# Later transposes between the stages, lo parts of just-in-time weights on GpSimd, and a bonus term computed one step later

## The chip, the cores and the metric

The kernel runs on one core of one Trainium2 chip, in one launch. The metric is the device time of that launch in microseconds (us), median of several runs. One execution was also profiled, and every duration below is from it.

## The reference

A batch of one sequence of 512 tokens with 1024 features goes through two transformer layers and then through one further block. All of it is float32.

```python
# layers i = 0 (latent and windowed attention), 1 (attention with forget gates)
x = layer_norm(ALPHA * x + mixer_i(x), ln1)            # mixer ends in  o @ w_out
x = layer_norm(ALPHA * x + relu(x @ w_up)**2 @ w_down, ln2)
x = x + sigmoid(x @ ple_w_gate + b) * (p[i] @ ple_w_proj)
# the second block
h = rms_norm(x); proj = h @ w_in
a = rwkv7(h, r, k, v)      # recurrence; adds bonus = sum_head(r * k * r_k) * v
c = conformer_conv(...)
x = x + (gate0 * (a @ w_rp) + gate1 * (c @ w_cp)) @ w_o
x = x + relu(rms_norm(x) @ w_ff1)**2 @ w_ff2
return rms_norm(x)
```

## The kernel before

**Numbers.** Each float32 product is made of three TensorE matmuls on rounded parts: hi x hi, hi x lo, lo x hi (`mm3`, line 285). Every weight tile (128 x 1024) is brought by SyncE's DMA queue into a `wraw` buffer, ScalarE writes its hi part, and the lo part, raw - hi, is made in one of two ways (`load_part`, line 257). Without a named engine, ScalarE writes -hi and GpSimd issues a DMA that adds raw to it (lines 266, 267). With one, that engine subtracts (line 269). `fast=True` takes VectorE and GpSimd in turn and overrides the named engine.

**Layout.** The residual x is token-major: four tiles of 128 tokens x 1024. A product needs its other operand feature-major, X = (hi, lo), 8 x 128 features by 512 tokens. `to_fm` (line 337) brings one token block there: 2 x 4 transposes on TensorE into two psum banks, then hi by ScalarE and lo by VectorE (lines 348, 349).

**Handovers.** A mixer ends in `out_proj` (line 534): four columns of 256, in each column four token blocks (one step = 24 matmuls of 256 columns), and an addition to x on VectorE per step. In the last column, `after(tb - 1)` follows step tb and `after(3)` follows the loop; `after` is a norm and then `to_fm` of that block (`norm_after`, line 551). `second_mixer` does the same by hand (lines 1254 to 1269), with all its transposes in the one bank psq. The next phase, `ffn` (line 400), begins with `up(0)`, whose two products are made in token halves (`halves=i == 0`, line 421); all its up-projection weights have their lo parts made by GpSimd (line 418). It ends in `down_last` (line 505), where `after(tb - 1)` follows the step of block tb, and `after(3)` follows `fill`, a small product of the gate phase. The gate phase (line 615) makes two columns of 512, the first with `fast`, the second through ScalarE and DMA.

**Recurrence.** In the second block eight feature chunks pass through four generators, a chunk a round further in each (lines 1211 to 1236): `wkv_proj`, `wkv_inputs`, `wkv_inverse`, `wkv_chunks`. `interleave` writes their steps in turn by the numbers they yield. `wkv_inputs` ends with the bonus (lines 1475 to 1480): r x r_k x k on VectorE, a sum per head on TensorE, and a product with v on VectorE. `wkv_inverse` inverts triangular blocks with a round trip through DRAM, and makes three token-major copies by transposes (lines 1554 to 1566); each has four copies out of psum, two on ScalarE and two on VectorE.

**Order.** The order in the program is a priority. A planner with a cost model places each instruction in its engine's queue, may move a ready one ahead of one that isn't ready, and inserts the semaphores; on the chip each engine takes its queue in order. Buffers of a tag (`bufs`) are handed on when their last reader is done.

Of the kernel before, what the change touches and what calls it, by code (L numbers as in the profile page):

```python
# [19 lines left out]
D = 1024  # L20
LOW = -3.0e38
DECAY_C = -0.5 * math.exp(-0.5)
HALVES = slice(0, 512), slice(512, 1024)


# [264 lines left out]

def proj_fm(g, W, X, m0, tag="psm", halves=False):

    ps = g.ps(tag)
    n = len(W)
    for t0, t1 in (((0, 256), (256, 512)) if halves else ((0, 512),)):
        for kc in range(n):
            w = tuple(a[:, m0:m0 + 128] for a in W[kc])
            mm3(g.nc, ps[:, t0:t1], w, (X[0][:, kc, t0:t1], X[1][:, kc, t0:t1]), kc == 0, kc == n - 1)
    return ps
# [36 lines left out]

def to_fm(g, src, X, tb, tag="psm"):

    nc = g.nc
    for half in range(2):  # L340
# [58 lines left out]

def ffn(g, w_up, w_down, X, alpha, hp, tmp, after, fill=None):  # L400

# [11 lines left out]
    QS = {k: hp.tile([128, 2, 512], F32, name=f"q{k}", tag=f"q{k}", bufs=1) for k in (5, 6, 7)}  # L413

    def up(i):

        plain = i // 2 == units - 1
        W = g.load_w(w_up[:, i * 256:i * 256 + 256], eng=nc.gpsimd)
        F = tmp.tile([128, 8, 256], F32, name="hf", tag="hf")
        for e in range(2):  # L420
            p3 = proj_fm(g, W, X, e * 128, halves=i == 0).rearrange("p (a t) -> p a t", a=2)
# [107 lines left out]
    if fill:  # L529
        fill()  # L530
    after(3)


def out_proj(g, w, Ws, X, alpha, tag, after, order=None):

    nc = g.nc
    for c in range(4):  # L540
        W = Ws[c] if c < len(Ws) else g.load_w(w[:, c * 256:c * 256 + 256])
        for tb in range(4):
            ps = proj_tm(g, W, X, tb, tag, order)
            xs = g.x[tb][:, c * 256:c * 256 + 256]
            nc.vector.scalar_tensor_tensor(xs, xs, alpha, ps[:, 0:256], op0=ALU.mult, op1=ALU.add)
            if c == 3 and tb > 0:
                after(tb - 1)
    after(3)


def norm_after(g, pool, l, which, X, tag):

    gb, bb = g.bcast_row(pool, f"{which}_g{l}", f"{which}g"), g.bcast_row(pool, f"{which}_b{l}", f"{which}b")

    def after(tb):
        layer_norm_tm(g, g.x[tb], gb, bb)
        to_fm(g, g.x[tb], X, tb, tag)

    return after


def ffn_and_ple(g, l, X):

    nc, tc, d = g.nc, g.tc, g.d
    with ExitStack() as s2:
# [16 lines left out]
        with ExitStack() as s3:  # L582
            hp = g.pool(s3, "hp", 3)
            tmp = g.pool(s3, "ftmp", 1)
            br = g.pool(s3, "brow", 1)
            after = norm_after(g, br, l, "ln2", X, "psm")
            P = []
# [4 lines left out]

            ffn(g, d[f"w_up{l}"], d[f"w_down{l}"], X, ALPHA, hp, tmp, after, fill)
        tmp = g.pool(s2, "ptmp", 3, side="right")
# [130 lines left out]
def even_mixer(g, outer, late, X, load_x):  # L725
    d, nc = g.d, g.nc
    with ExitStack() as st:
# [25 lines left out]
        for j in order:  # L753
            split_sb(g, OT[:, j, :], X[0][:, j, :], X[1][:, j, :], nc.vector)
        out_proj(g, d["ev_w_out"], W, X, ALPHA, "pss", norm_after(g, g.pool(st, "evn", 1), 0, "ln1", X, "pst"), order)

# [229 lines left out]
def odd_mixer(g, late, X):  # L986
    nc, tc, d = g.nc, g.tc, g.d
    with ExitStack() as st:
# [55 lines left out]
        g.weight_pools(late, *FFN_W, side="right")  # L1044
        out_proj(g, d["od_w_out"], W, X, ALPHA, "pss", norm_after(g, g.pool(st, "odn", 1), 1, "ln1", X, "pst"))

# [4 lines left out]
def first_block(g):  # L1051
# [22 lines left out]
    with ExitStack() as st:  # L1074
        g.small = g.pool(st, "small", 6)
        for l in range(2):
            with ExitStack() as late:
                if l == 0:
                    even_mixer(g, st, late, X, load_x)
                else:  # L1080
                    odd_mixer(g, late, X)
                ffn_and_ple(g, l, X)

# [12 lines left out]
def second_mixer(g, outer):  # L1096
    nc, tc, d = g.nc, g.tc, g.d
    H = g.X
    with ExitStack() as st:
# [150 lines left out]
        g.small = g.pool(outer, "small2", 6, side="right")  # L1250
        hn = g.pool(st, "hn2", 2)
        gb = g.bcast_row(hn, "norm_ff")

        def after(tb):
            ht = hn.tile([128, D], F32, name="hn2", tag="hn2")
            rms_norm_tm(g, g.x[tb], ht, gb, g.v1[:, V1["eps6"][0]:V1["eps6"][1]])
# [4 lines left out]
        for cc in range(4):  # L1261
            W = g.load_w(d["w_o"][:, cc * 256:cc * 256 + 256]) if cc else W
            for tb in range(4):
                ps = proj_tm(g, W, H, tb, ("psm", "pst")[tb % 2])
                xs = g.x[tb][:, cc * 256:cc * 256 + 256]
                nc.vector.scalar_tensor_tensor(xs, ps[:, 0:256], 0.5, xs, op0=ALU.mult, op1=ALU.add)
                if cc == 3 and tb > 0:
                    after(tb - 1)
        after(3)


# [133 lines left out]
def wkv_inputs(g, fc, st, env):  # L1405
# [81 lines left out]
def wkv_inverse(g, fc, st, env):  # L1487
# [198 lines left out]
def second_block(g, out):  # L1686
    nc, tc, d = g.nc, g.tc, g.d
    with ExitStack() as st:
        with ExitStack() as s2:
            g.psum(s2, psm=3, psd=1, pst=2, psq=1, pso=1)  # L1690
            second_mixer(g, st)
        g.psum(st, psa=4, psu=2, psm=2)
# [4 lines left out]

        def after(tb):
            ht = tmp.tile([128, D], F32, name="hn2", tag="hn2", bufs=3)
# [3 lines left out]

        ffn(g, d["w_ff1"], d["w_ff2"], g.X, 1.0, hp, tmp, after)

# [20 lines left out]
```

## Time and profile before

| | |
|---|---|
| median of 3 runs | 2544.66 us (2542.65 to 2544.73) |
| profiled execution, its own time | 2543.96 us |
| its span, first to last instruction | 2542.2 us |
| TensorE busy | 94% |
| VectorE, ScalarE, GpSimd busy | 60%, 50%, 40% |

The profile names PE (TensorE), PEld (its weight loads), DVE (VectorE), ACT (ScalarE), POOL (GpSimd) and SP (SyncE). A wait is put down to the work that released it. PEclk is the TensorE clock that was granted, 1.00 being the full 2.4 GHz.

### The profile page before, as it was taken

How to read it: one execution, taken by the hardware profiler on the slowest of the kernel's cores; microseconds unless marked ns; L12 is line 12 of the kernel's file. 1: busy time of each engine (PE TensorE's matmuls, PEld its weight loads, DVE VectorE, ACT ScalarE, POOL GpSimd, SP SyncE). 2: the span in 40 equal slices, each digit the busy share in tenths (PEclk: the TensorE clock that was granted, in tenths of full speed). 3: DMA queues.
4: the chain of work that ended last, by engine and by line, in shares of the span. 5: the costliest groups of instructions: out<-in, count | busy, mean ns of one | idle time of the engine just before them, and what ended most of it. 6: DMA issues, size and time to landing. Idle time of an engine off the chain costs nothing.

```text
span 2542.2 us, 36431 instructions
## 1 busy us (share of the span) xinstructions
PE 2381.3 (94%) x14140; PEld 1909.5 (75%) x14140; DVE 1531.6 (60%) x2834; ACT 1273.4 (50%) x1963; POOL 1028.3 (40%) x567
## 2 busy tenths in 40 slices
PE   8998999999999998999999988999998999799998
PEld 6778777787777787877877866777766778677776
DVE  3775464667343646565684697877767542555656
ACT  5782544445455644444445443555556533354543
POOL 1113667661011024767621332323354223367672
PEclk9999999999999999999999998999999999899999
DMA  7455232336555262232363565656675459132422
GB/s 207 89 154 162 67 112 88 108 123 158 147 125 122 62 166 88 71 121 79 115 171 93 123 151 124 150 130 136 137 175 145 133 171 258 41 116 73 125 70 82
DMA packets 303214, 315.35 MB, mean 124 GB/s; under 512 B 61376, under 2 KB 235072, under 8 KB 302912
## 3 DMA queue, kind: packets, MB, share of 16 engines
q1 hardware_dynamic: 280432, 239.60, 31.1%
q0 software_dynamic: 22032, 71.31, 15.6%
q8 instruction: 111, 1.82, 0.3%
q10 hardware_dynamic: 576, 2.10, 0.2%
q14 instruction: 63, 0.52, 0.1%
HBM read 221.47 MB, written 20.19 MB: 95 GB/s over the span
## 4 chain that ended last, share of the span: by engine, by line
PE 54%; DVE 15%; issue 9%; POOL 8%; DMA 8%; ACT 6%; SPq 0%; POOLq 0%; DVEq 0%; ACTq 0%
PE psm L286 7%; PE psm L287 7%; PE psm L288 7%; DMA wlo<-wraw 4%; PE psa L286 3%; PE psa L287 3%; PE psa L288 3%; POOL wlo L386 3%; DVE hl L386 2%; PE pst L1385 2%; PE psd L286 2%; DVE cacc L1376 2%; PE psd L288 2%; PE pss L287 2%; PE pss L288 2%
## 5 line engine op out<-in xcount | busy, mean ns | idle before, releaser
L286 PE MATMUL psm<-xT,whi 128*128 128x512 f32 (+1 forms) x1288 | 505.6, 393 | 20.8 <-DVE ksl L721 9.0
L287 PE MATMUL psm<-xT,whi 128*128 128x512 f32 (+1 forms) x1288 | 498.9, 387 | 1.4 <-DVE xT L349 1.4
L288 PE MATMUL psm<-xT,wlo 128*128 128x512 f32 (+1 forms) x1288 | 496.6, 386 | 3.0 <-DMA wlo<-wraw 3.0
L267 POOL DMA_DIRECT2D wlo<-wraw x153 | 132.6, 868 | 834.3 <-ACT wlo L266 560.3
L263 ACT ACTIVATE whi<-wraw 128x1024 fp32r<-128x1024 f32 (+3 forms) x287 | 286.2, 1005 | 334.8 <-PE psa L288 101.1
L386 POOL TENSOR_TENSOR wlo<-wraw,whi 128x1024 fp32r<-128x1024 f32 x84 | 214.3, 2552 | 282.9 <-ACT whi L385 282.9
L269 POOL TENSOR_TENSOR wlo<-wraw,whi 128x1024 fp32r<-128x1024 f32 x112 | 291.3, 2631 | 60.8 <-ACT whi L263 60.3
L286 PEld LDWEIGHTS psm<-xT,whi 128*128 128x128 f32 x1288 | 246.6, 192 | 73.5 <-issue 12.0
L288 PEld LDWEIGHTS psm<-xT,wlo 128*128 128x128 f32 x1288 | 247.0, 192 | 50.8 <-DMA wlo<-wraw 4.1
L287 PEld LDWEIGHTS psm<-xT,whi 128*128 128x128 f32 x1288 | 247.7, 192 | 46.8 <-DVE xT L349 2.6
L286 PE MATMUL psa<-whi,hh 128*128 128x512 f32 x600 | 239.1, 399 | 17.2 <-DVE x L443 17.0
L287 PE MATMUL psa<-wlo,hh 128*128 128x512 f32 x600 | 236.7, 395 | 0.0
L288 PE MATMUL psa<-whi,hl 128*128 128x512 f32 x600 | 236.5, 395 | 0.0
L385 ACT ACTIVATE whi<-wraw 128x1024 fp32r<-128x1024 f32 x147 | 151.6, 1053 | 127.0 <-PE psa L288 62.1
L1376 DVE SCALAR_TENSOR_TENSOR cacc<-glu,cw,cacc 128x512 f32<-128x512 f32 x240 | 199.4, 831 | 5.4 <-ACT cacc L1373 1.3
L386 DVE TENSOR_TENSOR hl<-hf,hh 128x768 fp32r<-128x768 f32 (+1 forms) x96 | 124.3, 1295 | 60.3 <-ACT hh L385 60.3
L385 ACT ACTIVATE hh<-hf 128x768 fp32r<-128x768 f32 (+1 forms) x96 | 87.7, 914 | 143.7 <-DVE hf L434 142.0
L286 PEld LDWEIGHTS psa<-whi,hh 128*128 128x128 f32 x600 | 112.8, 188 | 51.9 <-DVE x L443 25.1
L386 DVE TENSOR_TENSOR wlo<-wraw,whi 128x1024 fp32r<-128x1024 f32 x63 | 90.7, 1464 | 94.3 <-ACT whi L385 80.2
L266 ACT ACTIVATE wlo<-whi 128x1024 fp32r<-128x1024 f32 (+2 forms) x153 | 146.3, 960 | 2.3 <-PE psm L288 0.8
L288 PEld LDWEIGHTS psa<-whi,hl 128*128 128x128 f32 x600 | 112.8, 188 | 27.3 <-DVE hl L386 0.7
L287 PEld LDWEIGHTS psa<-wlo,hh 128*128 128x128 f32 x600 | 112.8, 188 | 25.8
(445 smaller groups left out, 5113.0 us busy)
## 6 DMA issues: line engine op xcount, KB each, us to landing
wlo<-wraw POOLq DMA_DIRECT2D x129, 512.0 KB, 5.4
wraw<-in_w_up SPq DMA_DIRECT2D x64, 512.0 KB, 4.5
wraw<-in_w_down SPq DMA_DIRECT2D x64, 512.0 KB, 3.5
wraw<-in_w_ff SPq DMA_DIRECT2D x64, 512.0 KB, 3.7
wraw<-in_w_in SPq DMA_DIRECT2D x56, 512.0 KB, 4.4
wraw<-in_od_w_in SPq DMA_DIRECT2D x24, 512.0 KB, 4.3
wraw<-in_ple_w_gate SPq DMA_DIRECT2D x16, 512.0 KB, 5.6
brow<-in_rows SPq DMA_DIRECT2D x13, 512.0 KB, 5.4
```

Of the source, the lines that this page charges most:

```text
L263: nc.scalar.activation(hi[:, :m], raw[:, :m], AF.Copy)
L266: nc.scalar.activation(lo[:, :m], hi[:, :m].bitcast(F32), AF.Copy, scale=-1.0)
L267: nc.gpsimd.dma_start(lo[:, :m].bitcast(F32), raw[:, :m], accum_op=ALU.add)
L269: eng.tensor_tensor(lo[:, :m], raw[:, :m], hi[:, :m].bitcast(F32), op=ALU.subtract)
L286: nc.tensor.matmul(ps, w[0], x[0], start=first, stop=False)
L287: nc.tensor.matmul(ps, w[0], x[1], start=False, stop=False)
L288: nc.tensor.matmul(ps, w[1], x[0], start=False, stop=last)
L385: g.nc.scalar.activation(hi, src, AF.Copy)
L386: (eng or g.nc.gpsimd).tensor_tensor(lo, src, hi.bitcast(F32), op=ALU.subtract)
L1376: nc.vector.scalar_tensor_tensor(acc, u[:, j:j + 512], cw[:, fc * 31 + j:fc * 31 + j + 1], acc, op0=ALU.mult, op1=ALU.add)
L1385: nc.tensor.matmul(ps[o], lhs[o], rhs[o], start=start, stop=stop)
```

## The change

In `out_proj` and `second_mixer` the columns 2 and 3 are made together for one token block, its norm follows at once, and the transposes follow two blocks later. The transposes of blocks 2 and 3 are returned as callables (`late`) and run inside the next phase: in `up(0)` between its half products, in the gate phase between its first steps. The first two up-projection weights take the way through ScalarE and DMA; weights of an output projection that are loaded inside the loop, and those of the second gate column, have their lo part made by GpSimd. In the recurrence, `wkv_inputs` makes only r x r_k x k, and sum and product run in `wkv_inverse` while its DRAM round trip is under way; the four copies per transposed tile all go to ScalarE. The buffers hn2 move to a longer-lived pool.

```diff
+LATE_TAGS = "pst", "psm"
+HALF_TOKENS = slice(0, 256), slice(256, 512)
 def ffn(...):                      # after -> late, norm, fm
+    def first_two(W):
+        pss = [g.ps("psm") for _ in range(2)]
+        for half, t in enumerate(HALF_TOKENS):
+            for e, ps in enumerate(pss):
+                for kc in range(8):
+                    w = tuple(a[:, e * 128:e * 128 + 128] for a in W[kc])
+                    mm3(nc, ps[:, t], w, (X[0][:, kc, t], X[1][:, kc, t]), kc == 0, kc == 7)
+                if half == 0:
+                    late[e]()
+        return pss
     def up(i):
-        W = g.load_w(w_up[:, i * 256:i * 256 + 256], eng=nc.gpsimd)
+        W = g.load_w(w_up[:, i * 256:i * 256 + 256], eng=nc.gpsimd if i > 1 else None)
     # down_last, behind the addition of block tb:
-                if c == 1 and tb > 0:
-                    after(tb - 1)
+                if c == 1:
+                    norm(tb)
+                    if fm and tb > 1:
+                        fm(tb - 2)
...
-    after(3)
+    return [functools.partial(fm, tb) for tb in (2, 3)] if fm else None
+def columns(g, w, Ws, step, norm, fm):        # out_proj and second_mixer call it
+    load = lambda c: Ws[c] if c < len(Ws) else g.load_w(w[:, c * 256:c * 256 + 256], eng=g.nc.gpsimd)
+    for c in range(2):
+        W = load(c)
+        for tb in range(4):
+            step(W, c, tb)
+    W2, W3 = load(2), load(3)
+    for tb in range(4):
+        step(W2, 2, tb)
+        step(W3, 3, tb)
+        norm(tb)
+        if tb > 1:
+            fm(tb - 2)
+    return [functools.partial(fm, tb, ("psa", "psa")) for tb in (2, 3)]
 # gate phase
-            Wg = g.load_w(d[f"ple_w_gate{l}"][:, cs], fast=c == 0)
+            Wg = g.load_w(d[f"ple_w_gate{l}"][:, cs], fast=c == 0, eng=nc.gpsimd)
             for tb in range(4):
+                if c == 0 and 0 < tb < 3:
+                    late[tb - 1]()
 # second_mixer: transposes of block tb
-            to_fm(g, ht, H, tb, "psq")
+            to_fm(g, ht[tb], H, tb, tags or (("psq", "pso"), ("psd", "psq"))[tb])
 # wkv_inputs
-    rk = tmp("tmpa")
-    nc.vector.scalar_tensor_tensor(rk, r, col(vv("r_k"), fc), k, op0=ALU.mult, op1=ALU.mult)
-    ps = g.ps("psm")
-    nc.tensor.matmul(ps, c("blk"), rk, start=True, stop=True)
     bon = new("bon", bufs=3)
-    nc.vector.tensor_tensor(bon, ps, v, op=ALU.mult)
+    nc.vector.scalar_tensor_tensor(bon, r, col(vv("r_k"), fc), k, op0=ALU.mult, op1=ALU.mult)
 # wkv_inverse, behind the issue of the round trip's last DMAs
+    ps = g.ps("psm")
+    nc.tensor.matmul(ps, c("blk"), st["bon"], start=True, stop=True)
+    nc.vector.tensor_tensor(st["bon"], ps, st["v"], op=ALU.mult)
+    yield 1.0
...
-                eng = nc.scalar.copy if hp == 0 else nc.vector.tensor_copy
-                eng(tv[64 * hp:64 * hp + 64, :, cp, :], p4[64 * cp:64 * cp + 64, :, hp, :])
+                nc.scalar.copy(tv[64 * hp:64 * hp + 64, :, cp, :], p4[64 * cp:64 * cp + 64, :, hp, :])
```

## Rows read from the trace of the kernel before

**Rows 1.** The page: busy time of each engine, share of the span, instructions.
```profile
PE 2381.3 (94%) x14140; PEld 1909.5 (75%) x14140; DVE 1531.6 (60%) x2834; ACT 1273.4 (50%) x1963; POOL 1028.3 (40%) x567
```

**Rows 2.** Stretches: us, busy us of each engine (instructions), PEclk, DMA share, GB/s.
```profile
210.00:218.00 8.00, 8.00 (x69) 8.00 (x68) 1.26 (x3) 1.06 (x1) 2.74 (x2) 1.00 0.90 255
...
2185.40:2193.40 8.00, 7.99 (x44) 7.99 (x45) 0.00 (x0) 0.00 (x0) 0.00 (x0) 0.61 0.17 61
...
226.00:257.00 31.00, 23.99 (x173) 21.86 (x172) 24.47 (x36) 10.38 (x17) 11.34 (x5) 0.94 0.11 33
...
1316.00:1328.00 12.00, 7.56 (x37) 5.10 (x36) 12.00 (x16) 6.57 (x11) 6.93 (x4) 1.00 0.87 216
...
2120.00:2140.00 20.00, 16.24 (x114) 15.74 (x113) 2.55 (x6) 8.98 (x10) 3.31 (x5) 0.83 1.05 285
...
640.00:650.00 10.00, 9.53 (x31) 7.26 (x32) 2.08 (x3) 0.63 (x1) 0.00 (x0) 0.73 0.84 195
...
1460.00:1480.00 20.00, 14.48 (x50) 10.58 (x50) 19.00 (x25) 7.91 (x11) 9.10 (x7) 0.83 0.68 150
```

**Rows 3.** TensorE's waits (total, times, longest): 226 to 257, 944 to 973, 2165 to 2203.
```profile
PE pst L344 <- issue: 3.3, 2, 1.8
PE pst L344 <- DVE bmv L368: 2.1, 1, 2.1
...
PE pst L344 <- DVE x L372: 2.7, 2, 1.4
PE pst L344 <- DVE bmv L368: 2.0, 1, 2.0
...
PE psq L344 <- DVE xT L349: 11.1, 4, 4.7
```

**Rows 4.** TensorE's waits, 900:916, 2120:2140, 630:650, 1354:1361; DMA landings (page, chain).
```profile
PE pss L287 <- DMA wlo<-wraw: 1.9, 2, 1.2
...
PE psm L287 <- DMA wlo<-wraw: 3.8, 2, 2.7
...
PE psa L287 <- DMA wlo<-wraw: 4.7, 3, 3.0
...
PE psa L287 <- DMA wlo<-wraw: 2.5, 2, 1.7
...
wlo<-wraw POOLq DMA_DIRECT2D x129, 512.0 KB, 5.4
...
2121.41 10.40 DMA wlo<-wraw
```

**Rows 5.** TensorE's waits at the two gates, 588 to 606 and 1316 to 1328.
```profile
PE psm L344 <- DVE x L372: 3.2, 2, 1.9
...
PE psm L344 <- DVE x L372: 3.5, 2, 1.8
```

**Rows 6.** TensorE's waits 1440 to 1560; line L1564, duration ns min/median/max.
```profile
PE psm L1478 <- DVE tmpa L1476: 5.5, 1, 5.5
PE pst L1557 <- DVE vtk L1564: 5.0, 1, 5.0
...
L1564 ACT COPY vtk<-pst x16: 348/369/371, 1519.1 to 2002.9; 64x256 f32<-64x256 f32 x16
...
L1564 DVE COPY vtk<-pst x16: 417/422/428, 1531.4 to 2003.3; 64x256 f32<-64x256 f32 x16
```

**Rows 7.** Timeline near 600 (start, us); line L371, duration ns min/median/max.
```profile
601.46 2.67 POOL L269 TENSOR_TENSOR wlo<-wraw,whi 128x1024 fp32r<-128x1024 f32 x1
...
590.08 1.41 DVE L372 SCALAR_TENSOR_TENSOR x<-x,rs,brow 128x512 f32<-128x512 f32 x2
...
601.55 3.80 DVE L372 SCALAR_TENSOR_TENSOR x<-x,rs,brow 128x512 f32<-128x512 f32 x2
...
L371 DVE SCALAR_TENSOR_TENSOR x<-x,bmv,brow x32: 727/747/2924, 223.5 to 1324.1; 128x512 f32<-128x512 f32 x32
```

More of the change, by code (lines that the diff above doesn't have):

```diff
@@ L1 @@
+import functools
 import itertools
@@ L288, in mm3, with proj_fm @@
     nc.tensor.matmul(ps, w[1], x[0], start=False, stop=last)
-def proj_fm(g, W, X, m0, tag="psm", halves=False):
+def proj_fm(g, W, X, m0, tag="psm"):
     ps = g.ps(tag)
     n = len(W)
[L295 to L298, printed above, removed]
+    for kc in range(n):
+        w = tuple(a[:, m0:m0 + 128] for a in W[kc])
+        mm3(g.nc, ps, w, (X[0][:, kc, :], X[1][:, kc, :]), kc == 0, kc == n - 1)
     return ps
@@ L334, in proj_tm, with to_fm @@
     return ps
-def to_fm(g, src, X, tb, tag="psm"):
+def to_fm(g, src, X, tb, tags=("psm", "psm")):
     nc = g.nc
-    for half in range(2):
+    for half, tag in enumerate(tags):
         ps = g.ps(tag)
@@ L397, with ffn @@
 BLOCK = {1: 0, 2: 1, 3: 6, 4: 2, 5: 3, 6: 4, 7: 5}
-def ffn(g, w_up, w_down, X, alpha, hp, tmp, after, fill=None):
+def ffn(g, w_up, w_down, X, alpha, hp, tmp, late, norm, fm=None, fill=None):
     nc = g.nc
@@ L530, in ffn, with out_proj, step, norm_fm @@
         fill()
-    after(3)
[L534 to L541, printed above, removed]
-        for tb in range(4):
[L543 to L551, printed above, removed]
-    gb, bb = g.bcast_row(pool, f"{which}_g{l}", f"{which}g"), g.bcast_row(pool, f"{which}_b{l}", f"{which}b")
[L555 to L562, printed above, removed]
+    return [functools.partial(fm, tb) for tb in (2, 3)] if fm else None
+def out_proj(g, w, Ws, X, alpha, tag, norm, fm, order=None):
+    def step(W, c, tb):
+        ps = proj_tm(g, W, X, tb, tag, order)
+        xs = g.x[tb][:, c * 256:c * 256 + 256]
+        g.nc.vector.scalar_tensor_tensor(xs, xs, alpha, ps[:, 0:256], op0=ALU.mult, op1=ALU.add)
+    return columns(g, w, Ws, step, norm, fm)
+def columns(g, w, Ws, step, norm, fm):
+    load = lambda c: Ws[c] if c < len(Ws) else g.load_w(w[:, c * 256:c * 256 + 256], eng=g.nc.gpsimd)
+    for c in range(2):
+        W = load(c)
+        for tb in range(4):
+            step(W, c, tb)
[7 more added lines that the diff above has]
+    return [functools.partial(fm, tb, ("psa", "psa")) for tb in (2, 3)]
+def norm_fm(g, pool, l, which, X, *tags):
+    gb, bb = g.bcast_row(pool, f"{which}_g{l}", f"{which}g"), g.bcast_row(pool, f"{which}_b{l}", f"{which}b")
+    return (lambda tb: layer_norm_tm(g, g.x[tb], gb, bb)), (lambda tb, own=tags: to_fm(g, g.x[tb], X, tb, own))
+def ffn_and_ple(g, l, X, late):
     nc, tc, d = g.nc, g.tc, g.d
@@ L585, in ffn_and_ple @@
             br = g.pool(s3, "brow", 1)
-            after = norm_after(g, br, l, "ln2", X, "psm")
+            norm, fm = norm_fm(g, br, l, "ln2", X, "psm", "psm")
             P = []
@@ L591, in fill @@
                 embed(0)
-            ffn(g, d[f"w_up{l}"], d[f"w_down{l}"], X, ALPHA, hp, tmp, after, fill)
+            late = ffn(g, d[f"w_up{l}"], d[f"w_down{l}"], X, ALPHA, hp, tmp, late, norm, fm, fill)
         tmp = g.pool(s2, "ptmp", 3, side="right")
@@ L754, in even_mixer @@
             split_sb(g, OT[:, j, :], X[0][:, j, :], X[1][:, j, :], nc.vector)
-        out_proj(g, d["ev_w_out"], W, X, ALPHA, "pss", norm_after(g, g.pool(st, "evn", 1), 0, "ln1", X, "pst"), order)
+        return out_proj(g, d["ev_w_out"], W, X, ALPHA, "pss", *norm_fm(g, g.pool(st, "evn", 1), 0, "ln1", X, *LATE_TAGS), order)
 def latents(g, a, X, W0):
@@ L1044, in odd_mixer @@
         g.weight_pools(late, *FFN_W, side="right")
-        out_proj(g, d["od_w_out"], W, X, ALPHA, "pss", norm_after(g, g.pool(st, "odn", 1), 1, "ln1", X, "pst"))
+        return out_proj(g, d["od_w_out"], W, X, ALPHA, "pss", *norm_fm(g, g.pool(st, "odn", 1), 1, "ln1", X, *LATE_TAGS))
 X_PARTS = ((0, 1), (1, 1), (2, 2), (4, 2), (6, 2))
@@ L1077, in first_block @@
             with ExitStack() as late:
[L1078 to L1082, printed above, removed]
+                last = even_mixer(g, st, late, X, load_x) if l == 0 else odd_mixer(g, late, X)
+                ffn_and_ple(g, l, X, last)
 def load_tokens(g):
@@ L1250, in second_mixer, with norm, fm, step @@
         g.small = g.pool(outer, "small2", 6, side="right")
-        hn = g.pool(st, "hn2", 2)
+        hn = g.pool(outer, "hn2", 2, side="right")
         gb = g.bcast_row(hn, "norm_ff")
-        def after(tb):
-            ht = hn.tile([128, D], F32, name="hn2", tag="hn2")
-            rms_norm_tm(g, g.x[tb], ht, gb, g.v1[:, V1["eps6"][0]:V1["eps6"][1]])
-            to_fm(g, ht, H, tb, "psq")
+        ht = {}
+        def norm(tb):
+            ht[tb] = hn.tile([128, D], F32, name="hn2", tag="hn2")
+            rms_norm_tm(g, g.x[tb], ht[tb], gb, g.v1[:, V1["eps6"][0]:V1["eps6"][1]])
+        def fm(tb, tags=None):
+            to_fm(g, ht[tb], H, tb, tags or (("psq", "pso"), ("psd", "psq"))[tb])
+        def step(W, c, tb):
+            ps = proj_tm(g, W, H, tb, ("psm", "pst")[(tb + c) % 2])
+            xs = g.x[tb][:, c * 256:c * 256 + 256]
+            nc.vector.scalar_tensor_tensor(xs, ps[:, 0:256], 0.5, xs, op0=ALU.mult, op1=ALU.add)
         W = g.load_w(d["w_o"][:, 0:256])
         g.weight_pools(outer, *FFN_W, side="right")
[L1261 to L1269, printed above, removed]
+        return columns(g, d["w_o"], [W], step, norm, fm)
 CONVS = (2, 1, 1, 1, 1, 1, 1, 0, 0)
@@ L1690, in second_block @@
             g.psum(s2, psm=3, psd=1, pst=2, psq=1, pso=1)
-            second_mixer(g, st)
+            late = second_mixer(g, st)
         g.psum(st, psa=4, psu=2, psm=2)
@@ L1696, in second_block, with norm @@
         gf = g.bcast_row(one, "norm_final")
-        def after(tb):
+        def norm(tb):
             ht = tmp.tile([128, D], F32, name="hn2", tag="hn2", bufs=3)
@@ L1702, in after @@
                 nc.sync.dma_start(out[tb * 128:tb * 128 + 128, h], ht[:, h])
-        ffn(g, d["w_ff1"], d["w_ff2"], g.X, 1.0, hp, tmp, after)
+        ffn(g, d["w_ff1"], d["w_ff2"], g.X, 1.0, hp, tmp, late, norm)
 def build(nc, tc, d, out):
```

3 lines of the change are left out of this document (2 added, 1 removed).

## The prediction

> **What bounds the kernel now.** I read the page first: TensorE is busy for 94% of the span, VectorE 60%, ScalarE 50%, GpSimd 40% [rows 1]. So TensorE's work sets the time, and a change can win only where TensorE stands still or runs at its lower clock. The second view, the table of stretches, says where that is. The stretches that the change touches are the handovers between phases and the recurrence of the second block. The reader should compare the stretch 210 to 218 us (69 matmuls of 256 columns in 8.0 us at a granted clock of 1.00, 0.116 us each) with 2185.4 to 2193.4 us (44 in 8.0 us at 0.61): after an idle stretch the engine also pays for the time in which it is granted the lower of its two levels, 1.2 instead of 2.4 GHz [rows 2]. I price that as busy time times (1 - granted clock). The third view, TensorE's waits by stretch, names the releasers: transposes that wait for a normalisation on VectorE [rows 3, 5], matmuls that wait for the DMA that accumulates a lo part [rows 4], and two long single waits in the recurrence [rows 6].
>
> **Transposes two blocks late, norms one step early.** No arithmetic is added. The same 4 norms and 8 groups of transposes run at each handover; what moves is when each becomes possible and what TensorE has in front of it.
>
> Before, in an output projection, all four norms start in the last column. TensorE then waits 3.3 + 2.1 = 5.4 us at the first handover, 2.7 + 2.0 = 4.7 at the second, and 11.1 at the third, where all transposes share the one psq bank [rows 3]; shorter waits are left out. The lower clock adds 24.0 x 0.06 = 1.4 us at the first, 8.0 x 0.39 = 3.1 at the third [rows 2], and I take 1.4 for the second, which is built like the first. Sum: 6.8 + 6.1 + 14.2 = 27.1 us.
>
> After, columns 2 and 3 are done together for one token block, so a norm can start every two steps, 2 x 24 matmuls x 0.116 = 5.6 us. A layer norm's four long VectorE instructions take 4 x 0.75 = 3.0 us when nothing disturbs them [rows 7]; two statistics passes over the same data and two short additions, by the same rate another 2 us, make about 5 us, which fits in 5.6, and three psum buffers give the matmuls over 5 us of slack behind it. Only the last block's norm is left when the projection ends. TensorE then has the transposes of block 1, two half products of the next phase (2.8 us each) and the transposes of block 2: some 7 to 8 us. Late next is that norm if GpSimd works beside it, for the lo parts of the third up-projection's weights come free at just that point. Undisturbed, 5 us are hidden; with two instructions locked (+2.2 each, below) it is 9.4 us, some 1.5 to 2 us late. The evacuation of block 3's transposes also stands between the last transposes and the second halves. In the third handover a wait is added: hn2 has two buffers, so block 2's norm (a ScalarE square first) needs block 0's transposes done. TensorE reaches those right after block 2's two steps, about when the square's input is ready; behind the square only later norms are queued, so I charge nothing beyond the allowance. I leave 2.5 us per handover: 27.1 - 7.5 = 19.6 us saved. Bounds: 0 (the norm chain still ends last) to 27.1.
>
> In the feed-forward's end the same is done towards the gate. There TensorE waits 3.2 and 3.5 us for norms [rows 5], but in the second of these stretches VectorE is busy for 12.00 of 12 us [rows 2]: it, not the order of TensorE's queue, is the limit, and none of its work goes. What helps is that the first two token blocks of the gate are now in front of the late transposes. I take half, 3.4 us; bounds 0 to 6.7.
>
> **Lo parts on GpSimd.** Before, ScalarE writes -hi, GpSimd issues an accumulating DMA and the sum lands 5.4 us later at the median, 10.40 us later in the busiest stretch [rows 4]. After, one GpSimd subtraction of 2.67 us does it [rows 7]. The TensorE waits that end on these DMAs are 1.9 us (second projection), 3.8 (third), 4.7 (first gate) and 2.5 (second gate) [rows 4]; with the lower clock, 16.2 x 0.17 = 2.8 in the third projection and 9.5 x 0.27 = 2.6 in the first gate [rows 2], 18.3 us in all. At 2.67 us a tile GpSimd is slower than the gate's matmuls eat tiles, so I leave 2.0 us in the first gate and 0.5 in the second: 15.8 us saved, bounds 0 to 18.3. In the third projection SyncE's queue gains too: its last weight transfer waits for a raw buffer that the accumulating DMA holds; released earlier, it is issued before columns 2 and 3 begin together and need both weights.
>
> The first two up-projections go the other way, to ScalarE and DMA: 4 ScalarE passes per feed-forward, on an engine that is busy 10.4 of 31 us there [rows 2]. The second one's buffers now come free only with the end of column 2, one step before the projection's end. Landing takes 5.4 us and four ScalarE passes of the same data as long again at most; TensorE meanwhile has four half products of 2.8 us and the transposes, over 11 us: hidden. Without that cover the whole would show, up to 10.4 us per feed-forward. The wait that the first projection has for its own second column's lo part is untouched, because that weight is loaded outside the changed line.
>
> **Bonus a step later, copies on ScalarE.** Per round the sum over a head on TensorE and the VectorE product behind it move from the inputs generator, where they wait for the k product, to the inverse generator, where their operand is a round old; they lie in the shadow of that generator's DMA round trip. The 5.5 us wait goes. The 5.0 us wait for VectorE's copy of vtk should go too, since 48 copies of 0.42 us leave VectorE [rows 6]. With the lower clock behind the first (14.5 x 0.17 = 2.5 us [rows 2]) and as much again behind the second, that is up to 15.5 us. But VectorE is busy 19.00 of 20 us in the first of these stretches [rows 2], so much of the wait will reappear as another. And four ScalarE copies in a row take 1.48 us where two pairs took about 0.84: 24 transposed tiles x 0.64 = 15.4 us if each lies on the path, while ScalarE is busy 7.91 of these 20 us. Nothing in the trace shows the new order, and the added pause in the generator shifts the order of everything beside it. From -15.4 to +15.5 I take +3, a little above the middle, because VectorE is the busier engine.
>
> **Sum.** 19.6 + 3.4 + 15.8 + 3.0 = 41.8 us. The profiled execution took 2543.96 us for a span of 2542.2; the 1.8 us around the span stay: 2543.96 - 41.8 = 2502 us. The median of the three runs shown is 0.7 us higher, so the same sum from there gives 2503.
>
> **A rule that speaks against it.** Beside a GpSimd subtraction of 2.67 us, two VectorE instructions of a norm took 3.80 us; without it the same pair takes 1.41, and single ones of the other pair range from 0.73 to 2.92 us [rows 7]. So one GpSimd instruction costs VectorE up to 2.2 to 2.4 us. The Trainium skill (SBUF — State Buffer, section "SBUF: two separate sides") says that a VectorE instruction with two SBUF inputs and a GpSimd instruction exclude each other for the whole of whichever starts first. The trace agrees: the pair is longer by nearly one whole GpSimd instruction. By that rule every part moved to GpSimd is a possible block.
>
> **The rivals.**
> 1. *The norm chain still ends last.* TensorE's new order doesn't help, because the last norms are slow on VectorE (12.00 of 12 us busy at the second gate). Only the lo parts pay: 2543.96 - 15.8 = 2528. For it: the locked norms in all three handovers. Against: the projections' first three norms now run while GpSimd has nothing to do.
> 2. *The recurrence loses.* ScalarE's copies in a row lengthen each round: 2543.96 - 38.8 + 15.4 = 2521. For it: ScalarE already waits there for VectorE's results and takes its work in order. Against: where the long waits are, it is busy 7.91 of 20 us and VectorE 19.00 [rows 2].
> 3. *The lock eats the gain: slower.* 4 + 6 + 6 parts in the three projections and 8 in the gates, 24 in all, come to GpSimd. If each blocks a norm that TensorE waits for, 24 x 2.2 = 52.8 us against 41.8 saved: 2543.96 + 11.0 = 2555. It decides from 19 of the 24 on. Against: in the projections most are made before the first norm starts, and 12 parts of the up-projections leave GpSimd.
> 4. *It doesn't do what it says.* The planner that orders each queue already pulls half products ahead of late transposes; if it orders the new program as the old, and the shorter lo parts only uncover the next wait, the time stays at 2544.
>
> **How the numbers follow.** The forecast, 2486 to 2518, has 0.54; a still larger gain, to 2476 (all upper bounds: 27.1 + 6.7 + 18.3 + 15.5 = 67.6), 0.03. Rival 1 has 0.17, rival 2 0.13, rival 3 0.07, rival 4 0.06. The range of 2478 to 2534 takes in the forecast and rivals 1 and 2, 0.84. What a measurement of this kernel can tell from no change is about 0.2%, 5 us. Faster by more than that are the forecast, the larger gain and rivals 1 and 2, less 0.01 for their edges: 0.86. Within it: rival 4 and that edge, 0.07. Slower: rival 3, 0.07.
>
> **What would show it.** In the changed profile the psq wait of the third handover should be gone, and the transposes of blocks 2 and 3 should stand between half products of the up-projection. Waits on the lo DMA should be left only in the first projection and the recurrence. The single waits of 5.5 and 5.0 us should be gone, and the recurrence (1440 to 2080 us) should keep its length within 15 us. The prediction is wrong if the handovers keep more than 3 us of idle each, if locked norms (3.5 us a pair) lie in front of TensorE's waits, or if the recurrence grows by more than 15 us.

## The result and the profile after

The changed kernel took 2507.8 us (median of 4 runs, 2501.2 to 2512.7), the kernel before 2543.7 us (4 runs, 2538.1 to 2544.7) beside it. The ratio is 0.9859, with a 95% interval of 0.9842 to 0.9875: 36 us or 1.4% faster. The forecast was 2502 with a range of 2478 to 2534. The total came out; how it is made up did not.

The table below cuts both executions at the same matmuls (first and last one into a psum tag or on an operand, times from the timeline). "First handover" runs from the end of the first mixer's attention to the first down-projection, and so contains the output projection and the first up-projections. A gate's row begins with the last matmuls into psu, near the end of the feed-forward. "Saved" is taken before rounding, from one execution of each kernel.

| us | before | after | saved | forecast |
|---|---|---|---|---|
| first handover | 102.3 | 95.3 | 7.0 | 4.3 |
| first gate, up to the second attention | 194.4 | 194.6 | -0.3 | 7.0 |
| second attention | 169.8 | 172.1 | -2.4 | 0 |
| second handover | 94.5 | 88.1 | 6.4 | 5.5 |
| second gate, up to the recurrence | 121.6 | 122.1 | -0.5 | 3.7 |
| recurrence | 682.6 | 680.2 | 2.4 | 3.0 |
| third projection and handover | 162.6 | 141.7 | 20.9 | 18.3 |
| the rest | 1014.6 | 1012.0 | 2.5 | 0 |
| span | 2542.2 | 2506.2 | 36.0 | 41.8 |

The forecast column splits the prediction's terms by place: order less 2.5 us each plus lo parts at the handovers, half of 3.4 plus the lo parts at each gate. All three handovers gave a little more than forecast, the recurrence about what was forecast, and both gates nothing. TensorE does take its work in the new order: at the first handover the late transposes start at 236.24 and 240.34 us, between half products of the up-projection that start at 232.66, 237.03 and 241.68.

Engine busy time on the page, as in [rows 1]:

```profile
PE 2366.2 (94%) x14140; PEld 1898.9 (76%) x14140; DVE 1517.9 (61%) x2786; ACT 1279.2 (51%) x1999; POOL 1042.2 (42%) x567
```

Stretches of the changed kernel that answer to [rows 2] (same columns): first handover, third handover, third projection, first gate, second gate.

```profile
218.60:249.60 31.00, 29.34 (x234) 27.86 (x233) 23.55 (x35) 14.24 (x22) 13.07 (x7) 1.00 0.44 113
...
2147.40:2155.40 8.00, 8.00 (x56) 7.87 (x56) 2.36 (x4) 1.43 (x3) 2.77 (x1) 0.80 0.85 223
2082.80:2102.80 20.00, 19.42 (x105) 16.60 (x104) 5.22 (x8) 5.60 (x7) 8.79 (x7) 1.00 0.89 249
...
567.60:617.60 50.00, 42.21 (x191) 33.86 (x190) 38.08 (x60) 19.77 (x28) 7.22 (x5) 0.93 0.55 150
1304.00:1316.00 12.00, 4.31 (x15) 2.74 (x15) 12.00 (x14) 6.10 (x9) 6.41 (x4) 0.64 0.87 206
```

At the first handover TensorE is busy for 29.34 of 31 us at full clock, where it was 23.99 at 0.94. At the second gate it is the other way: 4.31 of 12 us at 0.64, where it was 7.56 at 1.00, with VectorE at 12.00 of 12 in both. TensorE's waits in the changed kernel (releaser: total, times, longest): the third handover, 2127.8 to 2168, the first gate, the second gate, and 1440 to 1560 in the recurrence, against [rows 3, 5, 6].

```profile
PE psa L347 <- DVE xT L352: 1.1, 1, 1.1
PE psm L290 <- DVE xT L352: 0.9, 1, 0.9
...
PE psa L291 <- DVE wlo L273: 6.2, 1, 6.2
PE psm L347 <- DVE xT L352: 2.5, 2, 1.5
...
PE psa L291 <- DVE wlo L273: 5.8, 1, 5.8
...
PE psd L290 <- DVE glu L1401: 4.4, 1, 4.4
PE psm L1473 <- DVE v L1122: 4.3, 1, 4.3
```

The 11.1 us on psq are down to some 2 us, on other banks. At both gates the waits on norms and on lo DMAs have turned into one new wait of about 6 us, on a lo part that VectorE makes (L273 is L269 of before). The timeline of the first gate shows why (start, duration, engine; a repeated instruction is one line):

```profile
571.49 1.06 ACT L267 ACTIVATE whi<-wraw 128x1024 fp32r<-128x1024 f32 x1 [6.29 <-PE psa L292]
572.89 1.06 ACT L267 ACTIVATE whi<-wraw 128x1024 fp32r<-128x1024 f32 x1 [0.34 <-PE psa L292]
...
592.04 0.86 POOL L271 DMA_DIRECT2D wlo<-wraw  x1 [26.83 <-ACT wlo L270]
592.60 4.97 POOL L273 TENSOR_TENSOR wlo<-wraw,whi 128x1024 fp32r<-128x1024 f32 x2
593.22 0.64 DVE L352 TENSOR_TENSOR xT<-psm,xT 128x512 fp32r<-128x512 f32 x1
593.84 4.95 DVE L374 SCALAR_TENSOR_TENSOR x<-x,bmv,brow 128x512 f32<-128x512 f32 x2
598.71 1.40 DVE L375 SCALAR_TENSOR_TENSOR x<-x,rs,brow 128x512 f32<-128x512 f32 x2
600.04 2.35 DVE L273 TENSOR_TENSOR wlo<-wraw,whi 128x1024 fp32r<-128x1024 f32 x2
...
601.30 0.79 PE L291 MATMUL psa<-wlo,xT 128*128 128x512 f32 x1 [6.22 <-DVE wlo L273]
```

The weight's first hi part is ready at 572.6. Its lo part on VectorE runs at 600.04, behind the last block's norm, of which one pair takes 4.95 us instead of 1.4 while GpSimd makes two other lo parts of the same weight. The first of these had its hi part by 574 (the second ScalarE line). It started only at 592.60, because GpSimd takes its queue in order: the accumulating DMA ahead of it, for a weight of the next mixer, left GpSimd idle for 26.83 us until ScalarE had written its -hi.

The second attention's loss of 2.4 us has a cause in the trace as well. The output projection's lo parts, now made by GpSimd, begin there while VectorE still works for the attention. VectorE's four instructions on sx take 3.38 us beside them, and TensorE waits for their result (the last line is the kernel before):

```profile
891.91 3.38 DVE L697 TENSOR_SCALAR sx<-sx,r 128x128 f32<-128x128 f32 x4
...
892.62 4.91 POOL L273 TENSOR_TENSOR wlo<-wraw,whi 128x1024 fp32r<-128x1024 f32 x2 [31.51 <-ACT whi L267]
...
PE pst L708 <- DVE sx L697: 1.9, 1, 1.9
...
898.74 1.27 DVE L665 TENSOR_SCALAR sx<-sx,r 128x128 f32<-128x128 f32 x4
```

### The profile page after: what moved, and what is told of

Read it like the earlier page. It is cut to its first block, busy times and chain, and to the rows that moved or that the text cites. A ratio compares the mean times of both kernels' runs of the same rounds, so it can differ in the third digit from the quotient of the medians.

```text
span 2506.2 us, 36411 instructions
## 1 busy us (share of the span) xinstructions
PE 2366.2 (94%) x14140; PEld 1898.9 (76%) x14140; DVE 1517.9 (61%) x2786; ACT 1279.2 (51%) x1999; POOL 1042.2 (42%) x567
## 4 chain that ended last, share of the span: by engine, by line
PE 48%; POOL 14%; DVE 13%; issue 12%; ACT 7%; DMA 6%; POOLq 0%; SPq 0%; DVEq 0%; ACTq 0%
PE psm L290 6%; PE psm L291 6%; PE psm L292 6%; POOL wlo L389 5%; DVE cacc L1406 3%; PE psa L290 3%; PE psa L291 3%; PE psa L292 3%; POOL wlo L273 2%; DMA wlo<-wraw 2%; PE pss L292 2%; PE pss L291 2%; PE pss L290 2%; PE psd L290 2%; PE pst L1415 1%
## 5 line engine op out<-in xcount | busy, mean ns | idle before, releaser
L271 POOL DMA_DIRECT2D wlo<-wraw x141 | 122.8, 873 | 740.0 <-ACT wlo L270 495.1
L273 POOL TENSOR_TENSOR wlo<-wraw,whi 128x1024 fp32r<-128x1024 f32 x124 | 321.2, 2627 | 83.3 <-ACT whi L267 79.6
L389 POOL TENSOR_TENSOR wlo<-wraw,whi 128x1024 fp32r<-128x1024 f32 x84 | 213.2, 2538 | 239.6 <-ACT whi L388 239.6
L270 ACT ACTIVATE wlo<-whi 128x1024 fp32r<-128x1024 f32 (+3 forms) x141 | 133.8, 952 | 2.3 <-PE psm L292 0.8
```

What stands on the lines that cost most here:

```text
L270: nc.scalar.activation(lo[:, :m], hi[:, :m].bitcast(F32), AF.Copy, scale=-1.0)
L271: nc.gpsimd.dma_start(lo[:, :m].bitcast(F32), raw[:, :m], accum_op=ALU.add)
L273: eng.tensor_tensor(lo[:, :m], raw[:, :m], hi[:, :m].bitcast(F32), op=ALU.subtract)
L389: (eng or g.nc.gpsimd).tensor_tensor(lo, src, hi.bitcast(F32), op=ALU.subtract)
```

## The experiments

Theory: the gates gained nothing because TensorE, rid of its wait for the transposes, now waits for the first gate weight's lo parts, which stand behind the norms on VectorE and whose GpSimd share holds the norms up. Rival: VectorE's whole work is the bound there and any wait comes back. All times are medians of 4 to 6 runs, and ratios are to the kernel before, run beside them (its medians were 2541.8 to 2544.2 us). Waits and segments are from one execution of each kernel.

**1. First gate column through ScalarE and DMA.**

```diff
-Wg = g.load_w(d[f"ple_w_gate{l}"][:, cs], fast=c == 0, eng=nc.gpsimd)
+Wg = g.load_w(d[f"ple_w_gate{l}"][:, cs], eng=nc.gpsimd if c else None)
```

> The lo parts of the first gate column go from VectorE and GpSimd in turn to ScalarE and the accumulating DMA; all else is as in the changed kernel (2507.8 us). Theory: both gates gained nothing because TensorE, no longer held by the transposes, now arrives at the gate while VectorE still works through the last norm, and the two lo parts on VectorE stand behind it (waits of 6.2 us at the first gate and 5.8 at the second). Then both waits go or shrink to 2 us, the long pair of the last norm (4.95 us) shrinks towards 1.4, and the time falls by 6 to 12 us, to 2496 to 2502. Rival: VectorE's whole work at that place is the bound; then the wait comes back as one for its evacuations of the transposes, and the time stays at 2506 to 2510.

Measured: 2494.9 us (2493.1 to 2496.6), ratio 0.9809 [0.9795, 0.9822], 13 us under the changed kernel, a little more than the 6 to 12 us expected. The two gate segments are 6.2 and 6.8 us shorter. TensorE's waits on lo parts at the first gate (588 to 606) and at the second:

```profile
PE psa L291 <- DMA wlo<-wraw: 0.2, 1, 0.2
...
PE psa L291 <- DMA wlo<-wraw: 3.2, 2, 2.1
```

The last block's pair on VectorE's timeline there:

```profile
595.17 1.40 DVE L374 SCALAR_TENSOR_TENSOR x<-x,bmv,brow 128x512 f32<-128x512 f32 x2
```

And the stretch that stands above for the changed kernel:

```profile
567.60:617.60 50.00, 49.77 (x233) 40.73 (x233) 35.49 (x63) 23.17 (x33) 6.06 (x7) 1.00 0.80 195
```

TensorE is busy for 49.77 us at full clock, where it was 42.21 at 0.93, and the pair takes 1.40. The theory holds; VectorE's whole work was not the bound. What this run does not tell is how much the same edit would give in the order of before: that kernel was not run.

**2. Both gates as before.** In `down_last` and `ffn_and_ple`:

```diff
-                if c == 1:
-                    norm(tb)
-                    if fm and tb > 1:
-                        fm(tb - 2)
+                if c == 1:
+                    if fm and tb > 0:
+                        norm(tb - 1)
+                        fm(tb - 1)
+                    elif not fm:
+                        norm(tb)
...
-            Wg = g.load_w(d[f"ple_w_gate{l}"][:, cs], fast=c == 0, eng=nc.gpsimd)
+            Wg = g.load_w(d[f"ple_w_gate{l}"][:, cs], fast=c == 0)
...
-                if c == 0 and 0 < tb < 3:
-                    late[tb - 1]()
```

> At the two gates alone the change is undone: norms and transposes of the feed-forward's end one block late as before, none handed on, second gate column through ScalarE and DMA. Theory: the gates' part of the change is worth nothing, since the waits only changed their name; 2506 to 2511 us, and the old waits on norms and on lo DMAs are back at both gates. Rival: it is worth what was forecast, 3.4 + 2.7 + 2.0 + 2.6 or about 10 to 11 us, and something else in the changed kernel lost them; then 2517 to 2520.

Measured: 2504.2 us (2502.6 to 2508.0), 0.9845 [0.9832, 0.9859]. The interval overlaps that of the changed kernel: the gates' part is worth nothing that can be told, and if anything a small loss (without it the time is a little below the 2506 to 2511 expected, and the gate segments are 1.4 and 2.1 us shorter). The old waits are back, at the first gate:

```profile
PE psa L291 <- DMA wlo<-wraw: 4.2, 2, 2.8
PE psm L347 <- DVE x L375: 3.2, 2, 1.9
```

**3. All gate lo parts on GpSimd.** As the first edit, with `eng=nc.gpsimd` for both columns.

> All lo parts of both gate columns on GpSimd, none on VectorE. It tells apart why the last norm and the lo parts behind it were late at the gates. If only the queue on VectorE is to blame (two lo parts of 1.2 us each behind the norms), the time falls as with the accumulating DMA, to 2494 to 2499. If GpSimd's instructions hold VectorE up (pairs of 3.8 to 4.95 us instead of 1.4 beside them), four of them in a row hold the last norm up longer, and are done 4 x 2.5 us after their start: 2503 to 2511, with waits of TensorE on GpSimd's lo parts of 4 us or more at each gate.

Measured: 2505.0 us (2501.0 to 2506.0), 0.9845 [0.9830, 0.9860]. The time is that of the second case, its waits are not: TensorE waits 2.0 us on GpSimd's lo parts at the first gate, and 5.3 us at each gate on norms. GpSimd and VectorE in the timeline of the first gate:

```profile
588.77 2.37 POOL L273 TENSOR_TENSOR wlo<-wraw,whi 128x1024 fp32r<-128x1024 f32 x1 [10.34 <-ACT whi L267]
592.18 2.40 POOL L273 TENSOR_TENSOR wlo<-wraw,whi 128x1024 fp32r<-128x1024 f32 x1 [1.04 <-ACT whi L267]
...
588.99 3.36 DVE L374 SCALAR_TENSOR_TENSOR x<-x,bmv,brow 128x512 f32<-128x512 f32 x2
592.28 3.52 DVE L375 SCALAR_TENSOR_TENSOR x<-x,rs,brow 128x512 f32<-128x512 f32 x2
```

The wait on norms (the same at either gate):

```profile
PE psm L347 <- DVE x L375: 5.3, 2, 3.5
```

Each GpSimd instruction that starts just ahead of a pair lengthens it by about 2 us. So taking lo parts off VectorE's queue is not enough; they have to leave GpSimd too.

**4. The same loads earlier.** The accumulating DMA for the first gate column, its first half loaded ahead of the norm of block 1:

```diff
     # down_last
+                    if fill and tb == 1:
+                        fill(0)
                     norm(tb)
...
+                wg = d[f"ple_w_gate{l}"][part * 512:part * 512 + 512, 0:512]
+                if part == 0:
+                    P.extend(g.load_w(d["pT"][l]))
+                    Wp0.extend(g.load_w(d[f"ple_w_proj{l}"][:, 0:512]))
+                Wg0.extend(g.load_w(wg))
```

> As the first run, and the loads of the first half of the first gate weight (and of the small product in front of it) come earlier in the program, ahead of the norm of block 1, so that the planner ranks their hi and lo parts above the norms. Theory: if the remaining wait is for the lo parts, it goes, and the time is 1 to 4 us under that of the first run: 2494 to 2500. Rival: the ScalarE passes now stand ahead of the norms' square roots and of the evacuations, and the last norm ends later: 2502 to 2508.

Measured: 2495.1 us (2489.4 to 2496.5), 0.9803 [0.9788, 0.9818]: not to be told from the first run. At the first gate only 0.2 us of lo DMA wait was left to take away; at the second the wait went from 3.2 to 1.5 us, too little to show in the time.

**5. Both gate columns through the DMA.** `Wg = g.load_w(...)` without an engine.

> Both gate columns through ScalarE and the accumulating DMA; the late order of the gates stays. Beside the run with only the first column so (2494.85 us) it tells what GpSimd's lo parts of the second column are worth. If they hide a wait that would come back (4.2 us at the first gate and 2.5 at the second, as where the gates were put back as before): 2501 to 2505. Rival: TensorE has by then enough in front of it, and GpSimd's parts beside the gate's VectorE work were worth nothing: 2493 to 2497.

Measured: 2503.7 us (2499.9 to 2507.1), 0.9848 [0.9834, 0.9862], 8.9 us over the first run and within the 2501 to 2505 of the first case. TensorE's lo DMA waits at the gates:

```profile
PE psa L291 <- DMA wlo<-wraw: 6.5, 3, 3.5
...
PE psa L291 <- DMA wlo<-wraw: 4.6, 4, 2.1
```

So the second column on GpSimd is worth 8.9 us once the first column is not in the way; the prediction's terms for it come to 7.3.

**6. The order of the output projections as before.** `columns` runs its four columns one after the other again, with norm and transposes one block late in the banks of before, and the first up-projection's half products run product by product (only the loop is shown):

```diff
-    W2, W3 = load(2), load(3)
-    for tb in range(4):
-        step(W2, 2, tb)
-        step(W3, 3, tb)
-        norm(tb)
-        if tb > 1:
-            fm(tb - 2)
+    for c in range(4):
+        W = load(c)
+        for tb in range(4):
+            step(W, c, tb)
+            if c == 3 and tb > 0:
+                after(tb - 1)
+    after(3)
```

> At the three output projections the order is put back: four columns one after the other, norms and transposes one block late, in the banks of before, and the first up-projection's half products product by product. The lo parts stay where the change put them, and so do gates and recurrence. Forecast: the order is worth 19.6 us, so 2507.8 + 19.6 = 2527 (2523 to 2531), and the waits of transposes on norms are back at all three handovers. Rival: most of the gain there comes from the lo parts (the order only uncovers them), 2510 to 2518. Second rival: the order is worth all that the handovers gained, about 32 us, 2537 to 2542.

Measured: 2532.9 us (2531.1 to 2535.3), 0.9959 [0.9945, 0.9972], 25 us over the changed kernel and 2 us above the band that was expected. The waits of before are back, here one from each handover:

```profile
PE pst L347 <- DVE bmv L371: 2.1, 1, 2.1
...
PE pst L347 <- DVE x L375: 2.1, 2, 1.3
...
PE psq L347 <- DVE xT L352: 11.7, 4, 4.8
```

**7. The lo parts of the output projections as before.** The new order stays.

```diff
-    load = lambda c: Ws[c] if c < len(Ws) else g.load_w(w[:, c * 256:c * 256 + 256], eng=g.nc.gpsimd)
+    load = lambda c: Ws[c] if c < len(Ws) else g.load_w(w[:, c * 256:c * 256 + 256])
```

> The weights that an output projection loads inside its loop have their lo parts made through ScalarE and the accumulating DMA again; the new order stays. Forecast: these lo parts are worth 1.9 us in the second projection and 3.8 + 2.8 in the third, so 2507.8 + 8.5 = 2516 (2513 to 2519). Rival: the new order needs the weights of columns 2 and 3 at the same time, so the old lo parts now delay it in all three projections: 2520 to 2530. Second rival: the new order hides them: 2506 to 2510.

Measured: 2530.1 us (2524.3 to 2533.4), 0.9945 [0.9931, 0.9959], 22 us over the changed kernel, as the first rival had it. The handover segments are longer by 3.8, 8.6 and 9.6 us. The second attention takes 169.8 us as before the change, and its 1.9 us wait on sx is gone. Waits in the second and third:

```profile
PE pss L291 <- DMA wlo<-wraw: 5.5, 3, 4.1
...
PE pst L291 <- DMA wlo<-wraw: 4.8, 3, 2.4
```

**8. The first two up-projections' lo parts on GpSimd.**

```diff
-        W = g.load_w(w_up[:, i * 256:i * 256 + 256], eng=nc.gpsimd if i > 1 else None)
+        W = g.load_w(w_up[:, i * 256:i * 256 + 256], eng=nc.gpsimd)
```

> The lo parts of the first two up-projection weights are made by GpSimd again, as before the change; all else is as in the changed kernel (2507.8 us). It tests the price that was put at nothing. If GpSimd's instructions (2.4 to 2.7 us) hold up the last block's norm at a handover, as they did at the gates, TensorE's last transposes are late by 2 to 4 us in each of three handovers: 2514 to 2520. Rival: the norms are done by then, and the two ways are worth the same: 2506 to 2510. Second rival: ScalarE, freed of four passes, evacuates the second up-projection earlier and its wait of 3 to 5 us shrinks: 2499 to 2505.

Measured: 2516.3 us (2513.8 to 2518.3), 0.9894 [0.9879, 0.9910], 8.5 us over the changed kernel. The time is that of the first case, its place is not: the second handover is 9.7 us longer, the first 0.9, and the third is 2.1 shorter. GpSimd and VectorE in the timeline of the second:

```profile
942.00 10.86 POOL L273 TENSOR_TENSOR wlo<-wraw,whi 128x1024 fp32r<-128x1024 f32 x4 [16.26 <-ACT whi L267]
...
942.24 5.67 DVE L375 SCALAR_TENSOR_TENSOR x<-x,rs,brow 128x512 f32<-128x512 f32 x2
953.33 3.48 DVE L375 SCALAR_TENSOR_TENSOR x<-x,rs,brow 128x512 f32<-128x512 f32 x2
```

And TensorE's longest wait there, for VectorE's evacuation (its copy out of psum) of block 1's transposes, which is queued behind the last norm:

```profile
PE psm L291 <- DVE xT L352: 8.5, 1, 8.5
```

**9 to 11. The recurrence.** Both parts put back, and each alone:

```diff
     # bonus: back into wkv_inputs, in wkv_inverse it goes
-    bon = new("bon", bufs=3)
-    nc.vector.scalar_tensor_tensor(bon, r, col(vv("r_k"), fc), k, ...)
+    rk = tmp("tmpa")
+    nc.vector.scalar_tensor_tensor(rk, r, col(vv("r_k"), fc), k, ...)
+    ps = g.ps("psm")
+    nc.tensor.matmul(ps, c("blk"), rk, start=True, stop=True)
+    bon = new("bon", bufs=3)
+    nc.vector.tensor_tensor(bon, ps, v, op=ALU.mult)
     # copies
-                nc.scalar.copy(tv[...], p4[...])
+                eng = nc.scalar.copy if hp == 0 else nc.vector.tensor_copy
+                eng(tv[...], p4[...])
```

> The bonus and the four copies per transposed tile are put back as they were before the change; the handovers, gates and lo parts stay. Theory: the recurrence's part of the change is worth the 2 to 4 us by which its stretch got shorter: 2510 to 2512. Rival: the stretch got shorter because of what stands around it (the projection weights that meet GpSimd there), and the bonus and the copies are worth nothing: 2506 to 2509. A second rival: each of the two is worth much and they work against each other; then the single waits of 5.5 and 5.0 us come back and the time is above 2514.

> Only the four copies per transposed tile are put back, two on ScalarE and two on VectorE; the bonus stays a step later. Both put back gave 2509.4 us, so together they are worth no more than 2 us. If each alone is worth nothing that can be told from the reordering of the recurrence: 2504 to 2511. Rival: they work against each other; if the copies on ScalarE lengthen the rounds, as feared, this kernel is faster than the changed one, 2493 to 2503, and the bonus put back alone is slower by as much.

> Only the bonus is put back to where it was; the four copies stay on ScalarE. The wait of 5.5 us for its product should be back. If another wait stands behind it anyway: 2504 to 2511. If that wait was a gain of its own, which the copies ate: 2512 to 2518. Rival: it runs the other way, the bonus a step later costs and the copies gain: 2496 to 2503.

| put back | us (range) | ratio, 95% interval | recurrence, us |
|---|---|---|---|
| nothing | 2507.8 (2501.2 to 2512.7) | 0.9859 [0.9842, 0.9875] | 680.2 |
| both | 2509.4 (2507.5 to 2512.8) | 0.9865 [0.9852, 0.9879] | 678.0 |
| copies | 2513.4 (2512.3 to 2521.3) | 0.9897 [0.9881, 0.9912] | 692.9 |
| bonus | 2503.2 (2500.5 to 2504.4) | 0.9845 [0.9831, 0.9858] | 678.0 |

Both together are worth nothing that can be measured, although with both put back the two single waits are there again (5.7 and 5.0 us, first fence). With the bonus late, the copies on ScalarE gain (5.6 us); with the copies on ScalarE, the late bonus gains nothing and may cost (4.6 us, intervals overlap). That is the last rival's direction. The last column is from one execution each, and the recurrence took 676.7 to 681.2 us in the nine other kernels here that don't touch it, so only 692.9 stands out; that execution took 2520.0 us, 6.6 above the median of its kernel, so part of the 692.9 may be its own. With only the bonus put back its wait is there again (second fence), and with only the copies put back the wait for vtk is (third):

```profile
PE psm L1508 <- DVE tmpa L1506: 5.7, 1, 5.7
PE pst L1588 <- DVE vtk L1595: 5.0, 1, 5.0
```

```profile
PE psm L1508 <- DVE tmpa L1506: 5.0, 1, 5.0
```

```profile
PE pst L1589 <- DVE vtk L1596: 4.2, 1, 4.2
```

**12. A follow-up.** The fourth run's edits, and two more:

```diff
-            p3 = (pss[e] if pss else proj_fm(g, W, X, e * 128)).rearrange("p (a t) -> p a t", a=2)
+            p3 = (pss[e] if pss else proj_fm(g, W, X, e * 128, "psa" if i == 1 else "psm")).rearrange("p (a t) -> p a t", a=2)
...
-        W.append(g.load_w(d["ev_w_out"][:, 256:512]))
+        W.append(g.load_w(d["ev_w_out"][:, 256:512], eng=nc.gpsimd))
```

> The early gate loads through the accumulating DMA (2495 us), and two waits that are older than the change taken away: the second weight column of the first output projection has its lo part made by GpSimd (wait of 6.3 us), and the second up-projection's products take psa banks, which stand idle there, in place of psm banks whose evacuation is late (waits of 3.3, 4.6 and 2.9 us). If all of it is idle time on TensorE: 2495 - 6.3 - 10.8 and 1 to 3 us for the lower clock, 2475 to 2479. Rival: the evacuations by ScalarE are the limit there and the wait moves to the next product: only the first is gained, 2485 to 2490. Second rival: the psa banks are then late for the first down-projection: 2490 or more.

Measured: 2482.6 us (2480.8 to 2483.6), 0.9759 [0.9745, 0.9773]: faster than both kernels, 12.5 us under the fourth run, between the first case and the rival. Its wait on the second weight column of the first projection, and what TensorE waits for around the first handover:

```profile
PE pss L291 <- POOL wlo L273: 0.6, 1, 0.6
...
PE psa L290 <- DVE x L458: 3.1, 2, 1.7
```

The 6.3 us wait is 0.6. The wait for psm banks is gone, but psa banks are waited for instead (3.1, 4.5 and 3.4 us at the three handovers), so that edit moved its wait, as the second rival had it, though not at that rival's price (2490 or more). From the first handover to the end of its feed-forward, where both edits act, the kernel is 8.4 us shorter than the fourth; in the second handover and feed-forward, where the banks act alone, 3.1, in the third 0.9. The two were not run apart.

## Why the prediction was right, and where it failed

**Gates: the step that failed.** "What helps is that the first two token blocks of the gate are now in front of the late transposes. I take half, 3.4 us; bounds 0 to 6.7." With the lo parts there, 10.7 us were forecast at the gates and none came (-0.8 by the segments). The blocks that were to cover the transposes are matmuls too, and need the first gate weight's lo parts. Two of these are made by VectorE, which the prediction itself read as busy for 12.00 of 12 us, and two by GpSimd. No term asked when they are done. Run 1 shows that these lo parts held the gates back: with them out of the way the two gate segments are 12.2 us shorter than before, more than forecast. How much of that is the new order and how much the way of the first column stays open, since the order of before was not run with this edit. One of the prediction's own signs of being wrong did show, a locked norm in front of a wait of TensorE: a pair of 4.95 us at the first gate. Rival 1's reading, VectorE ends last, was right at this one place, but what was late behind the norms was a weight and not a transpose. Pairs of 1.4 us took 3.36 to 5.67 us beside GpSimd's subtractions in runs 3 and 8 and in the changed kernel. The rule that the prediction took from the Trainium skill (SBUF — State Buffer, section "SBUF: two separate sides"), that a VectorE instruction with two SBUF inputs, as in these pairs, and a GpSimd instruction exclude each other, bears on this, and these traces agree with it.

**Handovers: right in sum, wrong as a sum.** Order (19.6) and lo parts (8.5) were added as if each stood alone: 28.1 forecast, 34.2 measured in the segments, less the 2.4 that the same lo parts cost the second attention, which no term named. Taken back singly they cost 25.1 and 22.3 us, which add up to more than both gave. By the segments the lo parts alone are worth 8.6 us (run 6 against before), as forecast, and the order alone 12.2 (run 7 against before), not 19.6: the rest comes only with both. In the second handover the order without the new lo parts even loses: 96.7 us against 94.5 before. The reason was partly named (columns 2 and 3 "need both weights"), but it was booked for the third projection alone; the first, booked at 0, is longer by 3.8 us without them. The idle time left is below the 3 us per handover that would have refuted the step only if the older wait for psm banks is left out: 1.5, 1.1 and 2.4 us. That wait, which no term had either, was 2.9 to 3.0 us before and is 3.3, 4.7 and 3.8 now; with it all three are above 3 us.

**Up-projections through ScalarE: right that they are hidden, but put at no gain.** Taken back, they cost 8.5 us. The "1.5 to 2 us late" for a locked norm was too small where GpSimd has four such parts in a row: TensorE waits 8.5 us, because an evacuation that TensorE needs is queued behind that norm.

**Recurrence: right by its middle, not by its reasons.** 3.0 forecast with 31 us between the bounds; 2.4 in the segment and 1.6 by the medians, which can't be told from nothing. Both single waits went and others of 4.4 and 4.3 us came, as the prediction allowed; with both edits put back the two waits return and the time stays, so they were worth next to nothing. The feared price of four ScalarE copies (15.4) did not show; the late bonus is the part without a gain. Whether that is its place or the order that the planner makes of the rest stays open.

**Total.** 41.8 forecast, 36.0 in the span. The gates lost 11.5 against the forecast, the second attention 2.4, and the handovers and the rest gave back what is left. That the total came out is luck: errors of both signs met in it.

## What to carry to other kernels

When a wait is taken from an engine, list every operand of the work that is to fill the gap and ask when it is ready: the filler's weights, too, are made by some engine, and if that engine is full the wait only changes its name. Two edits that serve one place (an order, and the weights it needs at once) are to be priced together: alone they gave some 12 and 9 us here, together 34, and in the second handover the order alone lost. Work that can run on three engines belongs on the one with slack in that stretch: lo parts gave 13 us when taken off VectorE and GpSimd at the gate's first column, and 8.9 us when left on GpSimd at its second.

## What the runs showed of the hardware

A GpSimd instruction delays a norm's VectorE pair by nearly its own length: in run 3 two of 2.37 and 2.40 us made pairs of 1.4 us take 3.36 and 3.52. It need not be an instruction with two tensors as inputs: four on sx alone went from 1.27 to 3.38 us. But not all of VectorE's work is held up: in the changed kernel an evacuation with one operand in psum took 0.64 us at 593.22, inside the 4.97 us in which the pair beside it went from 1.4 to 4.95. And ready GpSimd work can stand for long behind the mere issue of a DMA: at the first gate a subtraction whose hi part was there by 574 us started at 592.60, once ScalarE had written the part that this DMA adds to.
